# The recurrence branch's output projection: from block products inside the gate pairs to a stage of its own with seven products

## Chip, cores and metric

One core of one Trainium2 chip runs the whole kernel. The metric is device time in microseconds (us), the median of the runs.

## What is computed

One residual block in float32, for 1024 tokens of 1024 channels. Both branches read the same normalised input; what matters here is the merge:

```python
xn = rmsnorm(x, norm1_g)
u = xn @ w_in                      # q, k, v, f, i, q_hg, g_hg, gate_sb, gate_hg
o_sb = merge_heads(stick_breaking_attention(q_sb, k_sb, v_sb))        # 1024 x 512
o_hg = merge_heads(rmsnorm(hgrn2(...), hg_norm_g)) * silu(g_hg)       # 1024 x 512
g_a, g_b = sigmoid(gate_sb + b_a), sigmoid(gate_hg + b_b)
merged = g_a * (o_sb @ w_o_sb) + g_b * (o_hg @ w_o_hg)
h = x + merged @ w_out
h = h + square(relu(rmsnorm(h, norm2_g) @ w_ff1)) @ w_ff2
out = rmsnorm(h, final_g)
```

The change touches `o_hg @ w_o_hg`, a 1024 x 512 by 512 x 1024 product.

## The kernel before

Everything is kept with channels on partitions and tokens along the row. A float32 product is made of three matmuls of 128 x 128 weights on 512 tokens (`three`, L570): each operand is split into a rounded high part and the rest, and high x high, high x low and low x high are summed in a PSUM bank. The splits are `hi_lo` (L165): a cast on ScalarE (ACT, L157), then a subtraction on VectorE (DVE, L162). `load` (L136) issues loads on SyncE (SP), one behind the other; an instruction whose buffer or data isn't there yet holds back those behind it on its engine. Within an engine the order is that of the tile layer: it follows the code, with added edges by `after`, and buffers come from fixed pools, two each for the raw weights (`raw`), their high and low parts (`whi`, `wlo`), eight PSUM banks, 10 half tiles and 40 slots.

The large projections take seven products of half-size blocks in place of eight, with sums of weight blocks and of input blocks (forms). The gates' weight sums are made in DRAM by accumulating DMAs that GpSimd (POOL) issues, paced through the attention (`gate_weight_sums`, L1334; the sums `tw` for the output stage follow there, `out_weight_sums`).

**Gate pairs** (`GatePair`, from L1598). A pair cb makes 128 columns of both gates. Pairs 8 and 9 (named `gX8`, `gX9`) hold the gate g_hg of the recurrence and finish its four heads `on` (`ohg`); pairs 0 to 7 hold g_a and g_b and merge. The order is 8, 9, 0, 4, 1, 5, 2, 6, 3, 7 (L1773). Each runs, in the order of `gates` (L1783):

- `x6`: product 6 into bank gX; DVE makes gu = pr + gX, pr being partial products loaded from DRAM (12 matmuls).
- `y5`: product 5 into bank gY. Then `next_pair` splits the next pair's weights (wg, raw tiles of 1024 columns; whi/wlo and tgh/tgl their parts) and loads the one after.
- `x7`: product 7 onto gX; DVE reads gY (pr <- gY - pr, `pr<-gY,pr` in the profile), then gX twice; ACT takes sigmoids.
- `late_half`: for pairs 0 to 7 a block of 12 matmuls `pyh` (`hg_product`, L1655): 128 columns of `o_hg @ w_o_hg` for half of the tokens, 4 heads x 3. Its weights `wor` are loaded and split per pair (woh, wol), its inputs `a_hg` are the split heads (ahgh, ahgl). DVE multiplies and adds into y, which came with the attention branch's part (yr).
- `y3`: product 3 onto gY, so gY must have been read; DVE takes gu <- gY - gu, ACT the sigmoid.
- `early_half`: the other `pyh` block, and the merged result y; `out` (L1735) splits it (msh, msl) and, for pairs 4 to 7, makes forms (fs, yr) for the output stage.

So a pair of 0 to 7 has six blocks of 12 matmuls, four of gates and two of pyh. Behind pair 7 stands the output stage: banks pwW0 to pwW3 with a first product each, then a second each, and DVE adds and subtracts them to the residual rows h0 to h7 in between. Its weights are loaded into the raw buffers as wout11r, wout21r, wout2r and so on.

Of the kernel before, what the change touches and what calls it, by code (L numbers as in the profile page):

```python
# [20 lines left out]
P = 128  # L21
# [3 lines left out]
KT = D // P  # L25
# [15 lines left out]
def kernel(  # L41
# [1240 lines left out]

    a_sb, a_hg = Split("asb"), Split("ahg")
    mgs = Acts("ms")
# [49 lines left out]
    def gate_weight_sums():  # L1334
# [45 lines left out]
        yield from both(gh_sum(1, (0, 0), (0, 1)), (next(outs) for _ in range(2)))  # L1380
        yield from both(gh_sum(3, (0, 1), (1, 1)), (next(outs) for _ in range(2)))
        yield from outs

    def gate_sum(t, cb):
# [209 lines left out]
    class GatePair:  # L1594
# [3 lines left out]
        def load(self):  # L1598
# [7 lines left out]
            load(r1[:, 4:8], W_IN[512:, gate_cols(1, cb)].rearrange("(k p) c -> p k c", p=P))  # L1606
            if cb >= KT:
                return
            self.wo = half(f"wor{cb}")
            load(  # L1610
                self.wo.rearrange("p (k c) -> p k c", k=4),
                W_OHG[:, cb * P : (cb + 1) * P].rearrange("(k p) c -> p k c", p=P),
            )

        def load_sums(self):
            cb = self.cb
            self.p = slot(f"pr{cb}")
            load(self.p.rearrange("p (k t) -> p k t", k=2), pd[cb])
            if cb >= KT:
                load_g1(cb)  # L1620
                return
            self.y = slot(f"yr{cb}")
            load(self.y.rearrange("p (k t) -> p k t", k=2), yd[cb])

        def split(self, behind=None):
# [4 lines left out]
                slot(f"{t}g{cb}", F32R)  # L1630
                if self is gates_in[0]
                else wpool.tile([P, 1024], F32R, tag=t, name=f"{t}g{cb}")
# [6 lines left out]
            self.w.update({5: (h[:, s0], l[:, s0]), 7: (h[:, s1], l[:, s1])})  # L1639
            if cb >= KT:  # L1640
                return
            h, l = (half(f"wo{n}{cb}", F32R) for n in "hl")
            hi_lo(h, l, self.wo)
            self.hg = h, l

        def product(self, i, ps, start):
            open_block("fill")
            wh, wl = self.w[i]
            for k in range(4):
# [3 lines left out]
                three(ps, wh[:, ws], wl[:, ws], xh, xl, start and k == 0, k == 3, True)  # L1653

        def hg_product(self, i):  # L1655
            open_block("fill")
            ps = bank(f"pyh{self.cb}_{i}")
            for _ in proj_half(ps, self.hg, a_hg.mov, 4, i):
                pass
            return ps  # L1660

# [8 lines left out]
        def gated(self, which, first, second):  # L1670
            h = 2 * (self.cb - KT) + which

            def rest(u2_sum):
                if which == 1:
                    muls(u2_sum)
                a_hg.put(h, ohg[h], u2_sum)

# [99 lines left out]
    def next_pair(n, m, behind):  # L1777
        n.split(behind)
        n.load_sums()
        if m:  # L1780
            m.load()

    def gates():  # L1783
# [805 lines left out]
```

## Time and profile before

| | |
|---|---|
| median of 3 runs | 1421.53 us (1421.43 to 1423.29) |
| profiled execution | 1422.69 us, span 1420.9 us |
| clock granted to TensorE | 0.999 |
| PE (TensorE) busy | 1408.7 us, 99% |
| DVE busy | 1053.7 us, 74% |
| ACT busy | 683.6 us, 48% |
| pyh, first to last matmul | 596.9 to 719.1 us |
| output stage starts | 719.48 us |

Times in the trace count from the span's start. A row of the timeline gives start, duration, engine, line, operation and the tiles (written<-read); the chain of work that ended last gives start, length and group; a row of a window gives its length, then busy time and instructions of PE, PEld, DVE, ACT and POOL, the clock, and the DMA engines' busy share.

### The profile page before, as it was taken

Reading aid. Unit: us, or ns where it says so; the run is one execution under the profiler, and the core shown is the slowest. Engines: PE = TensorE matmul, PEld = TensorE weight load, DVE = VectorE, ACT = ScalarE, POOL = GpSimd, SP = SyncE. Lnnn points to the kernel's source line nnn. Section 1 sums busy time; section 2 is a strip of 40 time slices with the busy share of each in tenths; the row PEclk is TensorE's granted clock in tenths of the full one; section 3 lists DMA queues with packets and bytes.
Section 4 is the critical chain, followed back from the end, with each engine's and each line's share of the span. In section 5 each row is a group of like instructions: output and inputs, shape, how many; then the busy total and the mean of one; then the engine's idle time right before and its main releaser. Section 6 shows DMA issues by size and latency. Waiting matters only on the chain.

```text
span 1420.9 us, 18818 instructions
## 1 busy us (share of the span) xinstructions
PE 1408.7 (99%) x6848; PEld 1183.8 (83%) x6848; DVE 1053.7 (74%) x1443; ACT 683.6 (48%) x1183; POOL 191.1 (13%) x384
## 2 busy tenths in 40 slices
PE   9999999999999999999999999999999999999997
PEld 8888888888888888888888888888888888888886
DVE  7578898978556877866788897676666667768765
ACT  6366676664243544433244764445444443433343
POOL 3023222212232231000000300000000000000042
PEclk9999999999999999999999999999999999999999
DMA  7145766548767996465585514444446964776824
GB/s 241 42 82 114 153 167 133 121 131 182 182 144 177 296 240 225 140 216 170 163 303 193 185 57 166 163 163 146 138 143 244 355 256 159 270 283 235 282 93 174
DMA packets 175636, 260.26 MB, mean 183 GB/s; under 512 B 27020, under 2 KB 101304, under 8 KB 175544
## 3 DMA queue, kind: packets, MB, share of 16 engines
q1 hardware_dynamic: 146056, 190.37, 39.8%
q0 software_dynamic: 24048, 57.16, 17.9%
q10 hardware_dynamic: 5440, 11.54, 2.3%
q8 instruction: 54, 0.88, 0.2%
q14 instruction: 38, 0.31, 0.1%
HBM read 190.86 MB, written 88.60 MB: 197 GB/s over the span
## 4 chain that ended last, share of the span: by engine, by line
PE 97%; DVE 1%; ACT 1%; DMA 0%; POOL 0%; issue 0%; SPq 0%; POOLq 0%; DVEq 0%; ACTq 0%
PE pm L129 21%; PE pX L129 9%; PE pW L129 6%; PE pY L129 6%; PE pjqk L129 6%; PE gX L129 4%; PE gY L129 4%; PE pga L129 4%; PE pjf L129 3%; PE pjq L129 3%; PE pys L129 3%; PE pji L129 3%; PE pyh L129 3%; PE pjv L129 3%; PE po L129 3%; PE z L129 2%
## 5 line engine op out<-in xcount | busy, mean ns | idle before, releaser
L157 ACT CAST whid<-w 128x1024 fp32r<-128x1024 f32 x30 | 31.6, 1054 | 154.7 <-PE pm L129 90.1
L831 DVE TENSOR_TENSOR_SCAN rm<-rm,bits 128x511 f32<-128x511 f32 (+7 forms) x72 | 87.4, 1220 | 17.6 <-ACT rm L809 17.4
L129 PE MATMUL pm<-wlod,sh 128*128 128x512 f32 x240 | 93.5, 389 | 0.0
L129 PE MATMUL pm<-whid,sh 128*128 128x512 f32 x240 | 93.4, 389 | 0.0
L129 PE MATMUL pm<-whid,sl 128*128 128x512 f32 x240 | 93.4, 389 | 0.0
L129 PE MATMUL pm<-tl,sh 128*128 128x512 f32 (+1 forms) x210 | 81.3, 387 | 0.0
L129 PE MATMUL pm<-th,sl 128*128 128x512 f32 (+1 forms) x210 | 81.3, 387 | 0.0
L129 PE MATMUL pm<-th,sh 128*128 128x512 f32 (+1 forms) x210 | 81.3, 387 | 0.0
L2205 POOL TENSOR_SCALAR fss<-fss 128x1 f32<-128x1 f32 x8 | 4.5, 562 | 562.0 <-ACT fsc L2200 561.5
L162 DVE TENSOR_TENSOR wlod<-w,whid 128x1024 fp32r<-128x1024 f32 x30 | 36.7, 1222 | 54.0 <-ACT whid L157 54.0
L162 DVE TENSOR_TENSOR sl<-sa,sh 128x1024 fp32r<-128x1024 f32 x56 | 68.3, 1219 | 0.0
L157 ACT CAST wTh<-pw 128x128 fp32r<-128x128 f32 (+3 forms) x96 | 44.0, 486 | 42.7 <-PE pw L132 39.0
L157 ACT CAST sh<-sa 128x1024 fp32r<-128x1024 f32 x56 | 57.2, 1046 | 6.7 <-DMA sa<-ad 6.7
L162 DVE TENSOR_TENSOR wTl<-pw,wTh 128x512 fp32r<-128x512 f32 (+2 forms) x96 | 50.0, 546 | 7.1 <-ACT wTh L157 4.7
L129 PEld LDWEIGHTS pm<-wlod,sh 128*128 128x128 f32 x240 | 45.0, 187 | 9.8 <-DVE wlod L162 0.4
L129 PEld LDWEIGHTS pm<-whid,sl 128*128 128x128 f32 x240 | 45.1, 188 | 9.4
L129 PEld LDWEIGHTS pm<-whid,sh 128*128 128x128 f32 x240 | 45.0, 188 | 9.4
L170 DVE TENSOR_TENSOR bt<-bt,rm 128x511 f32<-128x511 f32 (+7 forms) x72 | 49.1, 685 | 4.0
L809 ACT ACTIVATE rm<-z 128x511 f32<-128x511 f32 (+4 forms) x96 | 48.2, 502 | 3.9 <-PE z L129 2.8
L129 PE MATMUL pX<-sqh,t1l 128*128 128x512 f32 x128 | 49.9, 390 | 0.0
L129 PE MATMUL pX<-sql,t1h 128*128 128x512 f32 x128 | 49.9, 390 | 0.0
L129 PE MATMUL pX<-sqh,t1h 128*128 128x512 f32 x128 | 49.8, 389 | 0.0
(894 smaller groups left out, 4447.8 us busy)
## 6 DMA issues: line engine op xcount, KB each, us to landing
w<-in_w_ff_dram SPq DMA_DIRECT2D x72, 512.0 KB, 4.7
sa<-ad SPq DMA_DIRECT2D x52, 512.0 KB, 6.2
tg<-in_w_in_dram POOLq DMA_DIRECT2D x35, 512.0 KB, 6.6
ad<-a SPq DMA_DIRECT2D x32, 256.0 KB, 4.5
ad<-s SPq DMA_DIRECT2D x16, 512.0 KB, 3.3
tw<-in_w_out_dram POOLq DMA_DIRECT2D x24, 256.0 KB, 7.2
pr<-pd SPq DMA_DIRECT2D x10, 512.0 KB, 6.7
x<-in_x_dram SPq DMA_DIRECT2D x8, 512.0 KB, 7.9
```

Source lines behind the costliest of these rows:

```text
L129: return pe(nc.tensor.matmul(*a, **k))
L157: hi_last[0] = after(in_turn("act", nc.scalar.copy(dst, src)), hi_behind[0])
L162: nc.vector.tensor_tensor(out=dst, in0=src, in1=hi.bitcast(F32), op=ALU.subtract),
L170: return nc.vector.tensor_tensor(out=out, in0=a, in1=b, op=ALU.mult)
L809: nc.scalar.activation(rm[:, s0 + c0 - 1 : s0 + m - 1], z[:, c0:m], AF.Sigmoid, scale=-0.125)
L831: sc = nc.vector.tensor_tensor_scan(out=rr, data0=rr, data1=bits[:, 1024 - nk + a : 1024 - nk + b][:, ::-1], initial=rm[:, b : b + 1] if i ...
L2205: nc.gpsimd.tensor_scalar(out=ssq, in0=ssq, scalar1=1.0 / D, scalar2=EPS, op0=ALU.mult, op1=ALU.add)
```

## The change

The pyh blocks, `wor` and `a_hg` go. In their place:

- `hg_weight_sums`: eight more accumulating DMAs of 512 KB each, which build sums of blocks of w_o_hg in DRAM (tv1 to tv4), one ahead of each of eight `tw` sums.
- `hg_forms`: the seven input forms, made out of the four heads in place on DVE (six subtractions, two additions) and split on ACT and DVE (hgh1 to hgh7, hgl1 to hgl7). Four of its steps are written behind gX0's `x6`, six behind `y5`, the rest behind product 3 of gY0.
- `hg_phase`, a stage behind the products of pair 0: four `HgPair`s (128 columns c and c + 512 each), every one with seven products of 2 x 3 matmuls into banks pyX, pyW and pyY; ACT copies bank contents (hp, hu, ht, hz), DVE combines them, and POOL and ACT store the four results per pair to DRAM (zd). Its weights are loaded as vb (6 x 128 columns) and va (8 x 128). The last products of HgPair 3 stand behind gX4's product 6.
- each gate pair loads its z (`zr`, 512 KB, on SP behind yr; pair 0's behind the first results, in `hg_phase`) and multiplies by it where it multiplied by pyh. Pair 4's weight parts are kept in slots.

A gate pair 1 to 7 so has four blocks of 12 matmuls, back to back: gX, gY, gX, gY. In the cut diff the class HgPair is left out but for its loads: per product it calls `three` for k = 0, 1, copies a bank on ACT (`kept`) and combines on DVE.

```diff
-    a_sb, a_hg = Split("asb"), Split("ahg")
+    a_sb = Split("asb")
...
+        yield from both(hg_weight_sums(), (next(outs) for _ in range(8)))
...
+    def hg_weight_sums():
+        def block(i, j):
+            return W_OHG[i * 256 : (i + 1) * 256, j * 512 : (j + 1) * 512]
+
+        for t, op, src in (
+            (1, ALU.bypass, block(0, 0)),
+            (3, ALU.bypass, block(0, 1)),
+            (1, ALU.add, block(0, 1)),
+            (3, ALU.add, block(1, 1)),
+            (2, ALU.bypass, tv[1]),
+            (2, ALU.add, block(1, 1)),
+            (4, ALU.bypass, tv[2]),
+            (4, ALU.add, block(1, 0)),
+        ):
+            paced(nc.gpsimd.dma_start(tv[t], src, accum_op=op))
+            yield
...
-            if cb >= KT:
-                return
-            self.wo = half(f"wor{cb}")
-            load(
-                self.wo.rearrange("p (k c) -> p k c", k=4),
-                W_OHG[:, cb * P : (cb + 1) * P].rearrange("(k p) c -> p k c", p=P),
-            )
...
-            self.y = slot(f"yr{cb}")
-            load(self.y.rearrange("p (k t) -> p k t", k=2), yd[cb])
+            if cb:
+                self.load_z()
+
+        def load_z(self):
+            self.y = slot(f"yr{self.cb}")
+            load(self.y.rearrange("p (k t) -> p k t", k=2), yd[self.cb])
+            self.z = slot(f"zr{self.cb}")
+            load(self.z.rearrange("p (k t) -> p k t", k=2), zd[self.cb])
...
-                if self is gates_in[0]
+                if self in (gates_in[0], gates_in[3])
...
-            h, l = (half(f"wo{n}{cb}", F32R) for n in "hl")
-            hi_lo(h, l, self.wo)
-            self.hg = h, l
...
-        def hg_product(self, i):
-            open_block("fill")
-            ps = bank(f"pyh{self.cb}_{i}")
-            for _ in proj_half(ps, self.hg, a_hg.mov, 4, i):
-                pass
-            return ps
...
-                a_hg.put(h, ohg[h], u2_sum)
+                    if h == 1:
+                        for _ in hg_split(1, (0, 1), 0):
+                            pass
...
-            ps = self.hg_product(1)
...
-            mul(p1, p1, ps)
+            mul(p1, p1, self.z[:, 512:1024])
...
-        def y3(self):
+        def y3(self, between=None):
             self.product(3, self.Y, False)
+            if between:
+                between()
...
-            ps = self.hg_product(0)
             y = self.y[:, 0:512]
-            mul(self.u2, self.u2, ps)
+            mul(self.u2, self.u2, self.z[:, 0:512])
...
+    def hg_split(m, heads, i):
+        if m not in hgf:
+            hgf[m] = tuple(slot(f"hg{n}{m}", F32R) for n in "hl")
+        for kk, h in enumerate(heads):
+            cs = slice(kk * 512, (kk + 1) * 512)
+            hi, lo = (t[:, cs] for t in hgf[m])
+            hi_lo(hi, lo, ohg[h][:, i * 512 : (i + 1) * 512])
+            yield
+
+    def hg_forms():
+        l, r = (cs for _, cs in halves())
+        yield from hg_split(2, (2, 3), 0)
+        yield from hg_split(4, (2, 3), 1)
+        for a, b in ((ohg[0], ohg[2]), (ohg[1], ohg[3])):
+            sub(b[:, r], a[:, r], b[:, r])
+            yield
+        for a in (ohg[0], ohg[1]):
+            sub(a[:, r], a[:, l], a[:, r])
+            yield
+        for a, b in ((ohg[0], ohg[2]), (ohg[1], ohg[3])):
+            sub(a[:, l], b[:, r], a[:, l])
+            yield
+        yield from hg_split(6, (0, 1), 0)
+        yield from hg_split(5, (2, 3), 1)
+        yield from hg_split(7, (0, 1), 1)
+        for a, b in ((ohg[0], ohg[2]), (ohg[1], ohg[3])):
+            add(b[:, l], b[:, l], a[:, l])
+            yield
+        yield from hg_split(3, (2, 3), 0)
...
+                (b[:, 0:4], W_OHG[:, c1]),
+                (b[:, 4:6], W_OHG[256:512, c2]),
+                (a[:, 0:4], tv13[:, c1]),
+                (a[:, 4:6], tv[2][:, c1]),
+                (a[:, 6:8], tv[4][:, c1]),
...
+    def hg_phase(v, n, m):
+        a, b, c, d = hgp
+        a.x1_w2()
+        a.x6_y5()
+        b.split_a()
+        c.load()
+        a.x7()
+        b.x1_w2()
+        c.split_b()
+        a.x4_y3()
+        v.load_z()
+        b.x6_y5()
+        c.split_a()
+        d.load()
+        b.x7()
+        c.x1_w2()
+        d.split_b()
+        b.x4_y3()
+        c.x6_y5()
+        d.split_a()
+        n.load()
+        c.x7()
+        d.x1_w2()
+        n.split()
+        n.load_sums()
+        m.load()
+        c.x4_y3()
+        d.x6_y5()
+        d.x7()
+        v.late_half()
+        v.early_half()
...
+            if v.cb == 0:
+                fs = hg_forms()
+                for _ in range(4):
+                    next(fs)
+                v.y5()
+                for _ in range(6):
+                    next(fs)
+                v.x7()
+                v.y3(lambda: [None for _ in fs])
+                hg_phase(v, n, m)
+                continue
+            if v.cb == 4:
+                hgp[3].x4_y3()
             v.y5()
-            if n and v.cb:
+            if v.cb == KT + 1:
+                next_pair(n, None, None)
+                hgp[0].load()
+                hgp[1].load()
+                hgp[0].split_b()
+                hgp[0].split_a()
+                hgp[1].split_b()
+            elif n:
                 next_pair(n, m, v.u2_sum if v.cb < KT else None)
-            elif not n:
+            else:
                 out_form["11"].split(1)
                 last_lo[0] = v.u2_sum
                 out_form["11"].split()
...
-            if not v.cb:
-                next_pair(n, m, v.y_sum)
```

Three places on DVE show what moves. The first is pair 0. Before, behind gX0's first reader (gu0), DVE finishes head on3 in two products, splits a head for `a_hg`, and reads gY0:

```order
L1289 TENSOR_TENSOR gu0_6024<-pr0_5961,gX0_6011 128x512
L170 TENSOR_TENSOR on3_5520<-on3_5520,gu9_5924 128x512
L170 TENSOR_TENSOR on3_5520<-on3_5520,pr9_5797 128x512
L162 TENSOR_TENSOR ahgl2_6027<-on2_5027,ahgh2_6026 128x1024
L1292 TENSOR_TENSOR pr0_5961<-gY0_6036,pr0_5961 128x512
```

After, from the same two products on3 on (gu0 stands one row ahead of them):

```order
L170 TENSOR_TENSOR on3_5538<-on3_5538,gu9_5941 128x512
L170 TENSOR_TENSOR on3_5538<-on3_5538,pr9_5816 128x512
L162 TENSOR_TENSOR hgl4_6066<-on2_5038,hgh4_6065 128x512
L162 TENSOR_TENSOR hgl2_6060<-on3_5538,hgh2_6059 128x512
L162 TENSOR_TENSOR hgl4_6066<-on3_5538,hgh4_6065 128x512
L1292 TENSOR_TENSOR on2_5038<-on0_4120,on2_5038 128x512
L1292 TENSOR_TENSOR on3_5538<-on1_4527,on3_5538 128x512
L1292 TENSOR_TENSOR on0_4120<-on0_4120 128x512
L1292 TENSOR_TENSOR on1_4527<-on1_4527 128x512
L1292 TENSOR_TENSOR on0_4120<-on2_5038,on0_4120 128x512
L1292 TENSOR_TENSOR on1_4527<-on3_5538,on1_4527 128x512
L1292 TENSOR_TENSOR pr0_5972<-gY0_6071,pr0_5972 128x512
```

Nine form operations (three splits, six subtractions in place) have come between on3 and the read of gY0, and the split of ahgl2 has gone.

The second is pair 2, behind pair 5. Before, from the first reader of gX2 to the read of gY2; wlog6, tgl6 and wol6 are low parts of pair 6's weights:

```order
L1289 TENSOR_TENSOR gu2_6515<-pr2_6420,gX2_6502 128x512
L162 TENSOR_TENSOR msl02_6260<-yr5_6307,msh02_6259 128x512
L162 TENSOR_TENSOR wlog6_6534<-wg6r1_6425,whig6_6533 128x1024
L1289 TENSOR_TENSOR yr5_6307<-yr5_6307,yr1_6180 128x512
L162 TENSOR_TENSOR tgl6_6538<-wg6r0_6424,tgh6_6537 128x1024
L162 TENSOR_TENSOR wol6_6542<-wor6_6429,woh6_6541 128x512
L1292 TENSOR_TENSOR pr2_6420<-gY2_6520,pr2_6420 128x512
```

After, the last twelve rows up to the same read; the two rows ahead of them are the first reader of gY5's last product (gu5) and yr5 times pr5:

```order
L1289 TENSOR_TENSOR yr5_6593<-yr5_6593,pr5_6591 128x512
L170 TENSOR_TENSOR gu5_6652<-gu5_6652,zr5_6595 128x512
L1292 TENSOR_TENSOR fs15_6707<-yr1_6496,yr5_6593 128x512
L1289 TENSOR_TENSOR yr5_6593<-yr5_6593,gu5_6652 128x512
L1292 TENSOR_TENSOR yr1_6496<-yr1_6496 128x512
L1289 TENSOR_TENSOR gu2_6745<-pr2_6676,gX2_6732 128x512
L1292 TENSOR_TENSOR yr1_6496<-fs15_6707,yr1_6496 128x512
L162 TENSOR_TENSOR msl02_6550<-yr5_6593,msh02_6549 128x512
L162 TENSOR_TENSOR wlog6_6764<-wg6r1_6683,whig6_6763 128x1024
L1289 TENSOR_TENSOR yr5_6593<-yr5_6593,yr1_6496 128x512
L162 TENSOR_TENSOR tgl6_6768<-wg6r0_6682,tgh6_6767 128x1024
L1292 TENSOR_TENSOR pr2_6676<-gY2_6750,pr2_6676 128x512
```

The split wol6 is gone; the end of pair 5's merge (yr5, fs15, yr1) stands closer, and its order around gu2 has changed. Pair 3 behind pair 6 reads the same but for one product less behind gu6; in pairs 1, 5, 6 and 7 at most one split of 1024 columns stands ahead of the read of gY.

The third is the change to the output stage. Before, the two splits of wout21r lie ahead of the reader of gY7's last product:

```order
L1289 TENSOR_TENSOR pr7_6789<-pr7_6789,gX7_6856 128x512
L162 TENSOR_TENSOR wout21l0_6983<-wout21r0_6978,wout21h0_6982 128x1024
L170 TENSOR_TENSOR pr7_6789<-pr7_6789,pyh7_1_6914 128x512
L170 TENSOR_TENSOR yr7_6791<-yr7_6791,pr7_6789 128x512
L162 TENSOR_TENSOR wout21l1_6987<-wout21r1_6980,wout21h1_6986 128x1024
L1289 TENSOR_TENSOR yr7_6791<-yr7_6791,pr7_6789 128x512
L1292 TENSOR_TENSOR gu7_6869<-gY7_6872,gu7_6869 128x512
```

After, that reader comes first:

```order
L1292 TENSOR_TENSOR gu7_7011<-gY7_7014,gu7_7011 128x512
L1289 TENSOR_TENSOR yr7_6957<-yr7_6957,pr7_6955 128x512
L162 TENSOR_TENSOR wout21l0_7099<-wout21r0_7094,wout21h0_7098 128x1024
L1292 TENSOR_TENSOR fs17_7059<-yr3_6860,yr7_6957 128x512
L170 TENSOR_TENSOR gu7_7011<-gu7_7011,zr7_6959 128x512
L1292 TENSOR_TENSOR yr3_6860<-yr3_6860 128x512
L1289 TENSOR_TENSOR yr7_6957<-yr7_6957,gu7_7011 128x512
L1292 TENSOR_TENSOR yr3_6860<-fs17_7059,yr3_6860 128x512
L162 TENSOR_TENSOR wout21l1_7103<-wout21r1_7096,wout21h1_7102 128x1024
L162 TENSOR_TENSOR msl03_6914<-yr7_6957,msh03_6913 128x512
L1292 TENSOR_TENSOR h4_7089<-h4_7089,pwW0_7109 128x512
L1289 TENSOR_TENSOR yr7_6957<-yr7_6957,yr3_6860 128x512
```

Both splits have moved behind the reader of gY7, the second by seven more operations. Behind these rows, in both kernels, stand the updates of h0, the two splits wout2l (whose loads use the buffers of the wout21 splits, in order), then the subtractions from h5 and h1 and the addition to h1 of bank pwW1.

On ACT the weight casts of the new stage stand among its copies: vbh3, hz1 and its store, whiv3, hu2 in this order, and later whig4, tgh4, hz2 and its store, hu3. On SP the order is that of `hg_phase`: yr0, zr0, vb3, va3, wg4r, pr4.

More of the change, by code (lines that the diff above doesn't have):

```diff
@@ L1381, in gate_weight_sums @@
         yield from both(gh_sum(3, (0, 1), (1, 1)), (next(outs) for _ in range(2)))
+        yield from both(hg_weight_sums(), (next(outs) for _ in range(8)))
         yield from outs
+    tv13 = dram("tv13", [512, 512])
+    tv = {1: tv13[0:256], 3: tv13[256:512]}
+    tv.update({i: dram(f"tv{i}", [256, 512]) for i in (2, 4)})
+    zd = [dram(f"zd{cb}", [P, 2, 512]) for cb in range(KT)]
+    def hg_weight_sums():
[13 more added lines that the diff above has]
+            yield
     def gate_sum(t, cb):
@@ L1639, in split @@
             self.w.update({5: (h[:, s0], l[:, s0]), 7: (h[:, s1], l[:, s1])})
-            if cb >= KT:
-                return
-            h, l = (half(f"wo{n}{cb}", F32R) for n in "hl")
-            hi_lo(h, l, self.wo)
-            self.hg = h, l
         def product(self, i, ps, start):
@@ L1781, in next_pair @@
             m.load()
+    hgf = {}
+    def hg_split(m, heads, i):
[26 more added lines that the diff above has]
+        yield from hg_split(3, (2, 3), 0)
@@ new lines @@
+    hgp = [HgPair(cp) for cp in range(4)]
+    def hg_phase(v, n, m):
[29 more added lines that the diff above has]
+        v.early_half()
@@ L1785, in gates @@
             v.x6()
-            v.y5()
-            if n and v.cb:
+            if v.cb == 0:
[11 more added lines that the diff above has]
+                hgp[3].x4_y3()
+            v.y5()
+            if v.cb == KT + 1:
[6 more added lines that the diff above has]
+            elif n:
                 next_pair(n, m, v.u2_sum if v.cb < KT else None)
-            elif not n:
+            else:
                 out_form["11"].split(1)
```

62 lines of the change are left out of this document (added).

## The prediction

> **What bounds the kernel now.** I read the chain of work that ended last first, whole and then for 560 to 720 us, which holds the first gate blocks up to the output stage.
>
> ```profile
> span 1420.9 us, 18818 instructions
> ...
> PE 97%; DVE 1%; ACT 1%; DMA 0%; POOL 0%; issue 0%; SPq 0%; POOLq 0%; DVEq 0%; ACTq 0%
> ```
>
> ```profile
> 567.16 2.72 PE gX L129 x12
> ...
> 586.20 2.72 PE gY L129 x12
> 588.92 2.72 PE gX L129 x12
> 591.64 2.72 PE gY L129 x12
> 594.36 2.72 PE gX L129 x12
> 597.08 2.72 PE pyh L129 x12
> 599.80 2.72 PE gY L129 x12
> ...
> 719.48 5.67 PE pwW L129 x25
> ```
>
> The second fence is that chain: start, length, group. Each block of 12 matmuls starts where the one before ends, so no other engine is waited for: 2.72 us per 12, or .2267 us per matmul. Two things must be seen. A matmul that goes is worth its full time; and an engine that answers late will show as a gap of PE, since here there is none.
>
> **What goes and what comes on PE.** The tile view of pyh counts what the change removes.
>
> ```profile
> L129 PE MATMUL pyh<-ahgh,woh x64: 389/389/389, 596.9 to 718.6; 128*128 128x512 f32 x64
> ...
> L129 PE MATMUL pyh<-ahgl,woh x64: 389/389/389, 597.1 to 718.9; 128*128 128x512 f32 x64
> ...
> L129 PE MATMUL pyh<-ahgh,wol x64: 389/389/389, 597.4 to 719.1; 128*128 128x512 f32 x64
> ```
>
> Three times 64, or 192 matmuls, 16 blocks: 16 x 2.72 = 43.52 us. The new stage has 4 column pairs x 7 products x 2 k x 3 = 168 of the same shape: 168 x .2267 = 38.08 us. **PE alone: -5.44 us.** A product of the new stage takes 6 x .2267 = 1.36 us.
>
> **What the new order makes PE wait for.** With the blocks packed closer, every answer of DVE and ACT is due earlier. I go through the places where PE reuses a bank or a form, taking each engine's order from the code and its durations from these rows (start, duration).
>
> ```profile
> 588.96 0.69 DVE L1292 TENSOR_TENSOR gu<-gY,gu 128x512 f32<-128x512 f32 x1 [0.46 <-PE gY L129]
> ...
> 592.56 0.69 DVE L170 TENSOR_TENSOR on<-on,gu 128x512 f32<-128x512 f32 x1
> 593.17 0.69 DVE L170 TENSOR_TENSOR on<-on,pr 128x512 f32<-128x512 f32 x1
> 594.51 1.23 DVE L162 TENSOR_TENSOR ahgl<-on,ahgh 128x1024 fp32r<-128x1024 f32 x1 [0.65 <-ACT ahgh L157]
> 595.65 0.69 DVE L1292 TENSOR_TENSOR pr<-gY,pr 128x512 f32<-128x512 f32 x1
> ```
>
> ```profile
> 579.34 0.60 ACT L157 CAST woh<-wor 128x512 fp32r<-128x512 f32 x1
> ...
> 591.25 1.06 ACT L157 CAST whig<-wg4r 128x1024 fp32r<-128x1024 f32 x1 [0.94 <-DMA wg4r<-in_w_in_dram]
> ```
>
> On DVE a 512-column operation is followed .60 later by the next and ends after .69; a 1024-column one 1.14 (594.51 to 595.65) and 1.22. On ACT a cast is .60 and 1.06; two 512 casts in a row end some .5 apart.
>
> *First gate block, the forms.* gY0's third product (form 3) may not start before DVE has read gY0 (pr0<-gY0). Before, that read ends at 596.34, and a pyh block still lies between: gY0 goes on at 599.80, 3.46 later. In the changed order both covers are gone. PE wants the bank at 597.08, right behind gX0; and ahead of pr0<-gY0 stand the nine form operations shown. Up to on3's second product DVE keeps its times (gu9, on2, one 1024-column split, gu9 by its sigmoid: 588.96 + .60 + .60 + 1.14 + .60 = 591.9, as before; so 593.17, ending 593.86). Then the two casts of on3 on ACT, .60 and .5: hgl2 at 594.5, hgl4 at 595.1; six differences at .60: 595.7 to 598.7; pr0<-gY0 at 599.3, ending 600.0. **Stall 2.9 us**, DVE work alone. If DVE could take pr0<-gY0 first, it would be 0, and the form-6 casts would be late instead.
>
> *Gate blocks 2 and 3.* A gate block was 16.3 us on PE with its pyh blocks; now it is 4 x 2.72 = 10.88, while DVE loses only the split of wor (.60).
>
> ```profile
> 620.00:719.50 99.50, 99.50 (x440) 82.39 (x439) 69.63 (x98) 31.63 (x43) 7.56 (x14) 1.00 0.56 183
> ```
>
> The third pair of columns is DVE: 69.63 us busy in 99.5, which is six blocks and a little. Less five wor splits that is 66.5 us of work, for six blocks of 10.88 = 65.3. So DVE has as much to do as PE, and its order decides. From the end of gY5's last product to the end of pr2<-gY2 stand 14 operations, two of 1024 columns: 11 x .60 + 2 x 1.14 + .69 = 9.6 us, while PE has gX2, gY2, gX2 to do, 8.16 us, before it wants gY2 back: 1.4. Two operations of which one needs the other's result lie .73 apart (718.40 to 719.13, below), which adds some .3: 1.7. From gY6's last product to pr3<-gY3 there are 13, hence 1.1. In pairs 1, 5, 6 and 7 at most one split of 1024 columns stands ahead of the read, and the sum stays under 8.16. **Stall 2.8 us.**
>
> *Out stage.* pwW1's second product may start when DVE has updated h1 with pwW1's first one. Five blocks behind gY7's end, P, it is due: P + 13.6. Ahead of that update DVE's order has the splits of wout2r, whose second load waits for the split of wout21 in the same buffer.
>
> ```profile
> 715.35 1.22 DVE L162 TENSOR_TENSOR wout21l<-wout21r,wout21h 128x1024 fp32r<-128x1024 f32 x1
> ...
> 717.09 0.68 DVE L1292 TENSOR_TENSOR gu<-gY,gu 128x512 f32<-128x512 f32 x1
> ...
> 718.40 0.69 DVE L1292 TENSOR_TENSOR yr<-yr 128x512 f32<-128x512 f32 x1
> 719.13 0.69 DVE L1292 TENSOR_TENSOR yr<-fs,yr 128x512 f32<-128x512 f32 x1
> ...
> 724.84 2.35 DVE L162 TENSOR_TENSOR wout2l<-wout2r,wout2h 128x1024 fp32r<-128x1024 f32 x2
> ...
> 728.30 0.68 DVE L1289 TENSOR_TENSOR h<-h,pwW 128x512 f32<-128x512 f32 x1
> ```
>
> ```profile
> 713.80 3.17 SPq L137 DMA_DIRECT2D wout2r<-tw  x2
> ```
>
> ```profile
> pr<-pd SPq DMA_DIRECT2D x9, 512.0 KB, 6.7
> yr<-yd SPq DMA_DIRECT2D x8, 512.0 KB, 6.6
> ...
> wor<-in_w_o_hg_dram SPq DMA_DIRECT2D x8, 256.0 KB, 5.1
> yd<-ys ACTq DMA_DIRECT2D x5, 256.0 KB, 4.1
> ...
> wout11r<-in_w_out_dram SPq DMA_DIRECT2D x2, 512.0 KB, 8.1
> ...
> wout2r<-tw SPq DMA_DIRECT2D x2, 512.0 KB, 6.6
> ...
> wg2r<-tg SPq DMA_DIRECT2D x1, 512.0 KB, 4.0
> ...
> wg4r<-in_w_in_dram SPq DMA_DIRECT2D x1, 256.0 KB, 3.4
> ```
>
> (The last is the list of DMA issues in 540 to 740: size, and us to landing.) Before, both wout21 splits stand ahead of gu7<-gY7, the second load of wout2r is issued as the second ends (713.80 + 3.17 less the issue itself), and h1 is done at 728.98, 4.1 ahead of 733.08. Now the second split stands eight operations behind P: .60 + .60 + 1.14 + 5 x .60 + 1.22 = P + 6.6. Load 6.6, cast 1.06, split 1.14, three updates 1.9: P + 17.3. **Stall 3.7 us.** With 4.0 for the load it is 1.1, with 8.1 it is 5.2.
>
> *The round trip of z.* The results go out to zd and come back as zr. The load of zr0 stands on SP ahead of vb3, va3 and wg4r, and waits until hz0's store has landed. From E, the end of the product that hz0 copies: copy .6, store 4.1, zr0's issue and two of vb3 1.0, vb3's landing 5.1 (wor is the same weights), then on ACT vbh3 .8, hz1 .5, whiv3 1.0, hu2 .6, and up to .7 for whiv2 ahead of hz0: E + 13.7 to 14.4. X2's product 7 waits for hu2 and is due ten products behind E, 13.6: .1 to .8. Then zr0 lands (6.6) and DVE, which stands at pr0<-zr0, does seven operations and the split wlov3 (5.7), which frees the buffer for wg4r's second load (.5 + 3.4); ACT casts both halves of it ahead of hu3: X3's product 7 is some 1.4 late. **I take 2.3 us**; with the shortest loads shown 0, with 1 us more for each of the four transfers 4.8.
>
> *vb1.* pr0 can be issued at gX8's end, 569.88; vb1's second part is issued when pr0 has landed (6.7) and lands at 581 to 581.7; vbh1, hgh2 and the sigmoid of gu8 follow on ACT (2.0), two operations on DVE (1.3), then gX9 goes on: 584.3 to 585 against 583.48, and .6 more at gY9. **I take 1.5 us**; 0 with loads of 4, 3.4 with 8.
>
> *Hidden.* The 8 sums of 512 KB on POOL move the last tw sums by eight places, in a stretch in which the DMA engines have no room:
>
> ```profile
> 480.00:520.00 40.00, 40.00 (x218) 34.38 (x217) 31.21 (x51) 17.89 (x39) 15.23 (x20) 1.00 1.03 270
> ```
>
> Their DMA share is 1.03, but PE does not idle, and the sums are read 60 us later: I take 0, from a gain of nothing to one block's loss of 2.7 if a transposed input comes late. The new copies on ACT lie under a busy share of a third.
>
> **Sum.** -5.44 + 1.5 + 2.9 + 2.8 + 2.3 + 3.7 = **+7.8 us**. Against the profiled execution (1422.69, 1.8 of it outside the span) that is 1430.5; the median of the runs shown stands 1.2 below it, so **1429.3**. Behind the out stage PE is the chain again, so nothing is given back.
>
> **Rivals.**
> *Fast loads.* If loads land like the fastest rows (4.0 and 3.4), vb1 and the round trip cost 0 and the out stage 1.1: -5.44 + 2.9 + 2.8 + 1.1 = +1.4, or 1422.9 on the median. Against it: the medians of nine, eight and two transfers are 6.7, 6.6 and 6.6, and zd, zr and the new weight loads add 9.6 MB net in the same stretch (4 + 4 + 3.6, less 2 of wor). The Trainium skill, "DMA: Bandwidth & Descriptors", section "Anatomy of one DMA — SWDGE (gpsimd) path", fits a transfer as about 2 us plus its bytes at 436 GB/s, an estimate of 3.2 us for 512 KB; by that rule the sum would be about +0.6; this trace's 6.7 for 512 KB disagrees. Chance .14.
> *The full gain: faster.* One mechanism: DVE's pr<-gY comes in time in blocks 0, 2 and 3, and loads are short. It decides at 597.08: if DVE has read gY0 by then and has no lag later, PE keeps its 24 matmuls: 1416.1. For it: DVE is busy 70% before the change. Against: six differences and two casts cannot fit between 593.86 and 597.08 (4.9 us of work). Chance .09; with only the forms' stall (-2.5, 1419.0) another .03.
> *Heavier traffic.* All the upper ends: -5.44 + 3.4 + 2.9 + 2.8 + 4.8 + 5.2 = +13.7, or 1435.2, and with the 2.7 of the sums 1438. Chance .08.
>
> **Chances.** Forecast .66 (1424.4 to 1434). About 0.2%, 2.8 us, is what a measurement of this kernel can tell from no change: faster .09, same .17 (fast loads and the forms alone), slower .74. The range 1420 to 1437 leaves out the full gain and the last of the heavy traffic, some .14.
>
> **What would show it.** Groups pyX, pyY and pyW of 168 matmuls in all in place of pyh; idle of PE ahead of gY0 released by DVE pr (2.9), of gY2 and gY3 by DVE pr (1.7, 1.1), of pwW by DVE h (3.7), of pyX by ACT hu (2.3), of gX9 and gY9 by DVE (1.5). The forecast is wrong if PE shows no idle at gY0, or if vb3, zr0 and wout2r land within 4 us.

## The result, and the profile after

The changed kernel takes **1436.3 us** (median of 4 runs, 1434.37 to 1439.62) against 1421.95 for the kernel before beside it: a ratio of 1.0102, 95% interval 1.0081 to 1.0122. So it is about 14 us slower, where 7.8 was forecast. The first lines of its page, span and chain:

```profile
span 1434.9 us, 18939 instructions
...
PE 86%; DMA 4%; DVE 4%; issue 2%; ACT 2%; POOL 1%; SPq 0%; POOLq 0%; ACTq 0%; DVEq 0%
```

PE held 97% of the chain before and holds 86% now; transfers, DVE and ACT have 10% of it. This is the path followed back from the end, not idle time: PE is busy for 1409.0 us, as long as before (1408.7) with 24 matmuls fewer. The place is found with five marks that both traces have (start of the matmul; the last column is the end of the last one):

| stage | before | after | difference |
|---|---|---|---|
| start to the last po (attention) | 327.8 | 326.8 | -1.0 |
| last po to the first gX | 228.2 | 234.9 | **+6.7** |
| first gX to the first pwW | 163.3 | 167.7 | **+4.4** |
| first pwW to the first pwX | 21.8 | 27.4 | **+5.6** |
| first pwX to the last matmul | 672.0 | 671.7 | -0.3 |

(Behind the last matmul 7.8 us follow before and 6.5 after, so the spans differ by 14.0.) Three stages lose time, and the first of them ends before any product of the new stage runs. What PE waited for in 340 to 760 us (us in all, times, longest); before, this view is empty over the same stretch:

```profile
PE gY L129 <- DVE pr L1292: 5.7, 4, 2.8
PE pwW L129 <- DVE h L1289: 3.7, 1, 3.7
PE pot L132 <- DVE hon L170: 3.3, 2, 2.5
PE sl L129 <- DVE q L170: 1.7, 1, 1.7
PE sl L129 <- ACT ksl L1067: 1.2, 1, 1.2
PE gX L129 <- DVE gu L1289: 0.4, 1, 0.4
```

The first two rows are the waits that were forecast; pot and sl lie in the recurrence, at 415 to 561 us, and were not. The pauses seen one by one, in the chain (start, length, group):

```profile
602.61 3.61 DVE on L1292 x6
606.23 0.61 DVE pr L1292
606.88 4.60 PE gY L129 x12
...
691.88 0.61 DVE pr L1292
692.54 3.01 PE gY L129 x12
...
714.96 0.61 DVE pr L1292
715.62 3.02 PE gY L129 x12
...
736.15 6.44 DMA wout2r<-tw
742.67 1.06 ACT wout2h L157
...
746.16 0.61 DVE h L1289
746.82 10.07 PE pwW L129 x36
```

Read them in pairs: six form operations and then pr0 ahead of gY0; pr2 and pr3 ahead of gY2 and gY3; wout2's load, its cast and h ahead of pwW. Two lengths are new: 12 matmuls behind the pause at gY0 take 4.60 us instead of 2.72, and 36 in pwW 10.07 instead of 8.16. The matmuls themselves, in the timeline behind gY0's pause:

```profile
606.88 0.50 PE L129 MATMUL gY<-gsh,whig 128*128 128x512 f32 x1 [2.78 <-DVE pr L1292]
...
608.22 0.63 PE L129 MATMUL gY<-gsl,whig 128*128 128x512 f32 x1
608.64 0.63 PE L129 MATMUL gY<-gsh,wlog 128*128 128x512 f32 x1
...
611.33 0.40 PE L129 MATMUL pyX<-hgh,vbh 128*128 128x512 f32 x1
611.56 0.39 PE L129 MATMUL pyX<-hgl,vbh 128*128 128x512 f32 x1
```

The slow ones follow each other by .43 instead of .23 (starts), and the granted clock of the windows (the third value from the end) says why:

```profile
606.90:608.90 2.00, 2.00 (x6) 1.63 (x7) 2.00 (x4) 1.86 (x4) 0.00 (x0) 0.66 0.05 12
608.90:611.00 2.10, 2.10 (x6) 1.64 (x6) 2.10 (x5) 1.53 (x3) 0.00 (x0) 0.51 0.00 0
```

The clock is halved for some seven matmuls: a pause of 2.78 us has cost 2.78 + 1.88, of which about .3 is the restart that every pause costs (last section).

The pause at 415 us, on POOL:

```profile
407.69 0.99 POOL L1404 DMA_DIRECT2D tv<-in_w_o_hg_dram  x1
...
415.25 0.52 POOL L1404 DMA_DIRECT2D tv<-tv  x1 [4.56 <-DMA tv<-in_w_o_hg_dram]
415.84 0.19 POOL L266 TENSOR_SCALAR hss<-hss 128x4 f32<-128x4 f32 x1
416.11 1.04 POOL L270 TENSOR_TENSOR hn_y<-hss,expo 128x4 f32<-128x4 f32 x1
```

The copy of tv1 into tv2 stands in POOL's queue until the sum issued at 407.69 has landed, at 414.97. Behind it stand hss and hn_y, the norm of a recurrence head, which DVE (hon) and then PE (pot) wait for.

The pauses at 527 and 533 us (sl) have another way. DVE stands at gs, which reads the transposed input xnl, and the operands q and k of sl come behind it on DVE:

```profile
523.90 1.23 DVE L1292 TENSOR_TENSOR gs<-xnl,xnl 128x1024 f32<-128x1024 f32 x1 [7.28 <-DMA xnl<-xnh]
```

Before, the same wait is 2.04. The slowest of the six transfers of xnl in this stretch takes 21.2 us from issue to landing, against 16.1 before and 14.6 in e9, and POOL now issues eight more tw sums between 506 and 542 us, next to these transfers. So of the 6.7 us 2.5 are a wait in POOL's queue and 2.8 (1.18 + 1.65) late transposed inputs; a pause of .79 at 561 and the restarts make the rest. That it is the tw sums that make xnl late is not shown by itself.

### The profile page after: what moved, and what is told of

The parts are those of the page before. It is cut to its first block, busy times and chain, and to the rows that moved or that the text cites. A ratio compares the mean times of both kernels' runs of the same rounds, so it can differ in the third digit from the quotient of the medians.

```text
span 1434.9 us, 18939 instructions
## 1 busy us (share of the span) xinstructions
PE 1409.0 (98%) x6824; PEld 1180.8 (82%) x6824; DVE 1071.6 (75%) x1474; ACT 699.5 (49%) x1210; POOL 198.0 (14%) x404
## 4 chain that ended last, share of the span: by engine, by line
PE 86%; DMA 4%; DVE 4%; issue 2%; ACT 2%; POOL 1%; SPq 0%; POOLq 0%; ACTq 0%; DVEq 0%
PE pm L129 21%; PE pX L129 9%; PE pW L129 6%; PE pY L129 6%; PE pjqk L129 5%; PE pga L129 3%; PE pji L129 3%; PE pjq L129 3%; PE pjv L129 3%; PE po L129 3%; PE pjf L129 3%; PE gY L129 3%; PE gX L129 2%; PE pwX L129 2%; PE z L129 2%; PE pw L132 2%
```

## The experiments

**Theory:** the 14 us are three things: pauses of PE where DVE's order puts other work ahead of the read that frees a bank; the half clock behind some of these pauses; and the eight weight sums, which hold up POOL's queue. **Rivals:** the bytes count and not the place of the sums; DVE is full, so that a pause taken away comes back later. Medians of the runs are given, but several edits are smaller than the spread of the changed kernel (1434 to 1440), so the stages decide. They are read from one profiled execution of each kernel. Last po to gX, gX to pwW, pwW to pwX, pwX to the last matmul:

| kernel | median us | ratio to before (95%) | po-gX | gX-pwW | pwW-pwX | behind |
|---|---|---|---|---|---|---|
| before | 1421.95 | | 228.2 | 163.3 | 21.8 | 672.0 |
| changed | 1436.3 | 1.0102 (1.0081 to 1.0122) | 234.9 | 167.7 | 27.4 | 671.7 |
| e1 sums left out | 1429.8 | 1.0050 (1.0035 to 1.0065) | 228.1 | 167.3 | 27.7 | 672.0 |
| e2 sums last | 1442.16 | 1.0141 (1.0124 to 1.0158) | 239.6 | 167.7 | 27.0 | 672.0 |
| e3 forms behind | 1436.57 | 1.0094 (1.0079 to 1.0109) | 236.8 | 163.7 | 25.7 | 672.0 |
| e4 pause filled | 1438.16 | 1.0113 (1.0096 to 1.0130) | 235.3 | 167.6 | 24.9 | 672.0 |
| e5 tg split behind | 1438.35 | 1.0107 (1.0093 to 1.0121) | 234.5 | 164.3 | 29.3 | 672.0 |
| e6 wout2 behind | 1436.9 | 1.0103 (1.0087 to 1.0118) | 237.4 | 165.8 | 21.8 | 675.2 |
| e9 sums early | 1430.71 | 1.0051 (1.0038 to 1.0065) | 228.0 | 167.3 | 25.0 | 672.0 |
| e10 = e9+e3+e5+e6 | 1425.72 | 1.0019 (1.0010 to 1.0028) | 228.0 | 161.2 | 21.8 | 677.9 |
| e11 wout2 in slots | 1433.49 | 1.0079 (1.0065 to 1.0093) | 236.3 | 165.6 | 23.7 | 672.0 |
| e12 = e9+e3+e5+e11 | 1424.97 | 1.0016 (1.0007 to 1.0025) | 228.2 | 160.4 | 24.8 | 672.0 |
| e13 = e12, whole split behind | 1423.09 | 1.0004 (0.9995 to 1.0013) | 228.0 | 161.6 | 23.4 | 672.0 |
| e14 = e13, wout2 split later | 1421.22 | 0.9987 (0.9978 to 0.9996) | 227.9 | 164.5 | 21.8 | 671.7 |

**e1, the sums left out.**

```diff
-        yield from both(hg_weight_sums(), (next(outs) for _ in range(8)))
...
-                (a[:, 0:4], tv13[:, c1]),
+                (a[:, 0:4], W_OHG[:, c2]),
...
```

> Leaves out the eight sums of w_o_hg's blocks (va is loaded from plain blocks of w_o_hg, so the new stage works with other weights); everything else is as in the changed kernel. Theory: PE's four gaps before the gate pairs (2.52 at 415, 1.18 and 1.65 around 530, 0.79 at 561: 6.1 us, none of them in before) come from these sums, which stand in POOL's queue ahead of the normalisation steps and of the transposed inputs' transfers. All four go: about 6 us less, some 1430. Rival: the gaps are what the execution happened to have, or come from the other transfers that were moved: they stay, and the time stays at 1436. The gaps at gY0, gY2, gY3 and pwW (2.8, 1.6, 1.0, 3.7) stay in both.

The stage up to gX is back at 228.1, and PE does not pause in it: the list of its waits from 340 to 560 us is empty (window: length, then PE's busy time; first the changed kernel, then e1):

```profile
440.00:560.00 120.00, 117.17 (x634) 99.87 (x633) 83.43 (x131) 58.35 (x130) 39.75 (x55) 1.00 0.94 244
```

```profile
440.00:560.00 120.00, 120.00 (x643) 102.21 (x642) 89.98 (x138) 63.70 (x137) 35.01 (x46) 1.00 0.92 243
```

The 6.7 us are the sums' own; the pauses at gY0 and in pwW stay.

**e2, the sums behind all others.**

```diff
-        yield from both(hg_weight_sums(), (next(outs) for _ in range(8)))
         yield from outs
+        yield from hg_weight_sums()
```

> The same eight sums, but behind all the sums of w_out instead of one ahead of each of eight. Theory (place in POOL's queue): the gap at 415, where a copy of tv1 into tv2 waits at the head of POOL's queue until the sum of tv1 has landed and a normalisation step waits behind it, goes (-2.5); around 530 the late transfers are now the sums of w_o_hg themselves, so those gaps may stay: 1431 to 1434. Rival (bytes): only the amount moved counts, the gaps add up to about 6 us as before, wherever they lie: 1436.

Both numbers missed: the pause at 415 is gone as the theory says, but the whole is slower, 1442.16. What PE waited for in 340 to 570, and POOL ahead of it:

```profile
PE pot L132 <- DVE hon L170: 9.2, 2, 8.7
```

```profile
551.09 0.51 POOL L1404 DMA_DIRECT2D tv<-tv  x1 [7.72 <-DMA tv<-in_w_o_hg_dram]
...
556.70 0.93 POOL L1404 DMA_DIRECT2D tv<-in_w_o_hg_dram  x1 [4.54 <-DMA tv<-tv]
...
558.27 0.19 POOL L266 TENSOR_SCALAR hss<-hss 128x4 f32<-128x4 f32 x1
```

With nothing between them, each sum waits at the head of POOL's queue for the one before to land (7.72, 4.54), and the norm of the last head stands behind the chain. The bytes are the same and the loss is 11.4 us instead of 6.7: it is the place and the chain that count.

**e9, the sums in the attention.** They are issued one every fourth step, where the DMA engines' share is .55 in the changed kernel and .61 now.

```diff
-        yield from both(hg_weight_sums(), (next(outs) for _ in range(8)))
...
+    hsums = hg_weight_sums()
...
         if i % 2 == 0:
             next(wsums, None)
+        if i % 4 == 1:
+            next(hsums, None)
```

> The eight sums of w_o_hg are issued one every fourth step of the attention, far ahead of the stretch in which the DMA engines are full; everything else is as in the changed kernel. Theory (place in POOL's queue, between the recurrence's normalisation steps): from the end of attention to the first gate pair the time falls from 234.9 to 228 us, the whole to about 1429.6, as with the sums left out, since the DMA engines have room there (share 0.55 up to 300 us). Rival (bytes): the sums delay the other sums, and the gaps come in the attention or again around 530: less than half of the 6.7 is won.

228.0 us up to gX, as with none, and 1430.71: met, and the rival by bytes falls. It takes both losses away at once, the wait in POOL's queue and the late inputs; no run parts the two.

**e3, forms behind product 7.**

```diff
                 v.y5()
+                v.x7()
                 for _ in range(6):
                     next(fs)
-                v.x7()
                 v.y3(lambda: [None for _ in fs])
```

> The six subtractions of the input forms are written behind product 7 of pair 0, so that DVE reads gY0 four operations after on3 instead of ten. Theory (DVE's order, and a clock that drops after such a pause): the gap ahead of gY0's product 3 (2.78) shrinks to under 0.5, and the twelve matmuls behind it take 2.7 us instead of 4.60: 4 to 4.7 us less, about 1432. Rival 1: the gap goes but the slow matmuls have another cause: 2.8 less. Rival 2: form 6 is now late and the same gap stands ahead of pyX0's product 6: no gain.

The pause at gY0 is gone and its block is 2.72; the stage from gX to pwW falls by 4.0, of which some .5 comes back at pyX0's product 7, where hu's copy stands on ACT behind six casts of the late forms (.21, the first of the two waits in the last row, and a restart):

```profile
603.95 2.72 PE gY L129 x12
```

```profile
PE gY L129 <- DVE pr L1292: 2.9, 3, 1.6
PE pwW L129 <- DVE h L1289: 2.0, 1, 2.0
PE pyX L129 <- ACT hu L1875: 0.5, 2, 0.3
```

The median does not show it (1436.57). The profiled execution lost as much more ahead of gX (3.6 in the attention, 1.9 behind it) as it won behind it, so the stage is the evidence here.

**e4, the pause filled** with 12 matmuls whose bank is not read.

```diff
                 v.x7()
+                spare = bank("spare")
+                v.product(7, spare, True)
                 v.y3(lambda: [None for _ in fs])
```

> Twelve matmuls more, a product 7 of pair 0 into a spare bank that nothing reads, between product 7 and product 3 of pair 0, where PE pauses for 2.78 us. Theory (the clock drops because PE pauses): the pause is filled, gY0's product 3 starts when it did, and its twelve matmuls take 2.72 instead of 4.60: 1.9 us less although 2.7 us of matmuls are added. Rival: they are slow for another reason (DVE's or ACT's reads, the bank): they stay at 4.60, and the time stays the same or grows by up to 2.7.

gY0's block takes 2.85 instead of 4.60 (starts of its first matmul and of the one behind its twelve):

```profile
608.14 0.50 PE L129 MATMUL gY<-gsh,whig 128*128 128x512 f32 x1
...
610.99 0.39 PE L129 MATMUL pyX<-hgh,vbh 128*128 128x512 f32 x1
```

But the stage is no shorter (pauses at gX9 and pyX were .4 and .9 longer here), nor is the median. And e5, e6 and e11 have the same pause of 2.78 or 2.79 at gY0 without a slow block; that alone makes their stage from gX to pwW 1.6 us shorter. So e4 agrees with the clock's account and does not settle it alone; the pauses of all the runs, in the last section, carry it.

**e5, the second split of the next weights behind the read of gY.**

```diff
-                next_pair(n, m, v.u2_sum if v.cb < KT else None)
+                if v.cb < KT:
+                    n.split(v.u2_sum, True)
...
             v.x7()
+            if n and v.cb < KT:
+                n.split_r0(v.y_sum)
+                n.load_sums()
+                if m:
+                    m.load()
```

> In gate pairs 0 to 7 the split of the first half of the next pair's weights (tgh, tgl) and the loads behind it are written behind product 7, so that one 1024-column split fewer stands on DVE ahead of the read of gY. Theory (DVE's order): 13 operations or 8.4 us stand against 8.16 of PE ahead of gY2, 12 or 7.8 ahead of gY3: the gaps there fall from 1.6 and 1.0 to 0.3 and 0, 2.3 to 3 us less between the first gate pair and the output stage. Rival (DVE is full over the whole stretch): the same operations come a little later and the gaps move to other pairs, as late products 6 or 5: no gain.

The pauses at gY2 and gY3 fall from 1.61 and 1.02 to .48 and .45, and the stage by 3.35 (1.6 of it because no slow block followed gY0's pause). But pwW's pause grew to 5.9 (wout2's second cast came 3.2 us after DVE was ready), and nothing is won in all:

```profile
PE pwW L129 <- DVE h L1289: 5.9, 1, 5.9
```

**e6, wout2 behind the updates of h.**

```diff
             if tb == 0:
-                out_operands(["2"])
                 load_rows(6, 2, 7, 3)
+            if tb == 3:
+                out_operands(["2"])
```

> The weights wout2 are loaded and split behind all four updates by pwW's first products instead of behind the first. Theory (the updates of h stand on DVE behind splits that wait for a load): the gap inside pwW (3.7, and 1.9 by the slow clock behind it) goes, and the stage from pwW to pwX falls from 27.4 to 22 us; 5.6 less. Rival: wout2 now comes late for pwX: the gap stands ahead of pwX instead, and the time stays.

pwW to pwX falls to 21.8, as forecast, and the rival is right too: 3.2 us come back behind it, since wout3's loads need the same two buffers.

```profile
PE pwX L129 <- DVE h L1292: 1.5, 1, 1.5
```

**e10, all of it.**

> All edits together: sums early, forms behind product 7 of pair 0, tg splits behind product 7 of the pairs, wout2 behind the updates. Theory: of the 14 us lost, 6.7 by the sums, 4.4 at gY0, 2.6 to 3 at gY2 and gY3 and 5.6 at pwW come back, and what stays is the change's own 24 matmuls less, -5.4, and 1 to 2 us of small gaps: 1417 to 1419, faster than both kernels. Rival (DVE full from the first pair to the output stage): the gaps come back elsewhere, and the time stays above 1422.

1425.72, above the forecast: 6 of the 14 us that were to come back moved behind pwX (677.9 instead of 672.0), as the rival says.

```profile
PE pwX L129 <- DVE h L1292: 1.7, 1, 1.7
PE hnt L132 <- DVE hn L2017: 1.7, 1, 1.7
```

**e11, wout2's raw weights in slots** (of which the forms' leave some free), so that their load no longer waits for wout21's split.

```diff
+            if n == "2":
+                out_form[n].roomy = (0, 1)
             out_form[n].split()
```

> The changed kernel, with wout2's raw weights loaded into two free slots instead of the two raw buffers that wout21 holds; the order of the code stays. Theory (the updates of h stand behind splits that wait for a load which waits for wout21's second split): the load comes early, DVE goes from that split through wout2's to the updates, P + 6.6 + 2.7 + 2.3 + 1.9 = P + 13.5 against 13.6: the gap in pwW goes from 3.7 to at most 0.5, pwW to pwX takes 22 us instead of 27.4, and the stages behind keep their 672 us, since nothing is moved behind: 5 us less. Rival 1 (the DVE work itself is late): a gap of 2 us or more stays. Rival 2: the time comes back behind pwX, as it did with the later split.

The pause in pwW is 1.65 instead of 3.71, pwW to pwX 23.7, and 672.0 behind it: nothing is pushed on. The median is 2.8 us lower where 5 were expected. Neither the theory's .5 nor the first rival's 2 us came, and the rest is not DVE's work, as that rival has it, but the load again:

```profile
729.66 10.62 DMA wout2r<-tw
```

```profile
740.14 2.52 DVE L162 TENSOR_TENSOR wout2l<-wout2r,wout2h 128x1024 fp32r<-128x1024 f32 x2 [1.27 <-ACT wout2h L157]
```

It is issued earlier and takes 10.62 us instead of 6.44, with the DMA engines' share at .99 in 729 to 741. DVE is idle for 1.27 of the 1.65 us, waiting for the cast of what it brings.

**e12 and e13.** e12 takes e9, e3, e5 and e11 together; e13 splits the other half of the next weights behind the read of gY too.

```diff
             self.y_sum = sub(p1, self.Y, p1)
+            if between:
+                between()
...
-                    n.split(v.u2_sum, True)
...
-            v.x7()
+            v.x7((lambda: n.split(v.y_sum, True)) if n and v.cb < KT else None)
```

> Sums early, forms behind product 7 of pair 0, tg splits behind product 7 of the pairs, and wout2 in slots at its old place in the code. Theory: 228 us up to the first gate pair, 161.2 from there to pwW, 22 to pwX, 672 behind: 2 us less than before in all, some 1419.5 to 1421. Rival: DVE's lag out of the gate pairs makes the updates late in pwW or pwX, as behind the later split (677.9 instead of 672): 1424 or more.

> As the kernel with sums early, forms behind, tg splits behind and wout2 in slots, but the other half of the next pair's weights (whi, wlo) is split behind DVE's read of gY too. Theory (order): the last gaps of 0.48 at gY2 and gY3 go, each with the 0.3 of a restart: 1.5 us less from the first pair to pwW, 159.7. Rival (DVE is as full as PE in the pairs): the next pair's product 6 waits for wlo instead, and the stretch stays at 161 or grows.

e12 missed at pwW (24.8 instead of 22), and its time is the rival's, 1424 or more. With e13 the pauses at gY2 and gY3 went, but two came at the next product 6 and behind it (.5 and .8), as its rival says, and the stage is no shorter:

```profile
PE pwW L129 <- DVE h L1289: 1.4, 1, 1.4
PE gX L129 <- DVE gu L1289: 0.8, 1, 0.8
PE gX L129 <- DVE wlog L162: 0.5, 1, 0.5
```

wout2's load takes 11.11 us in e13's chain (716.71 on), when the DMA engines are full (share 1.01 in 717 to 732), and 11.83 in e12's. Ahead of its splits DVE is idle for .97 us in e13 and 1.67 in e12, so of the pauses in pwW (1.37 and 2.70) an estimated 1.0 and 1.7 are the load and .4 and 1.0 DVE's own lag.

**e14, loaded there but split behind the updates.**

```diff
-                out_operands(["2"])
+                out_form["2"] = out_unit("2", tw[2])
+                out_form["2"].roomy = (0, 1)
+                out_form["2"].load()
                 load_rows(6, 2, 7, 3)
+            if tb == 3:
+                out_form["2"].split()
```

> As the kernel with sums early, forms behind, both halves of the next pair's weights split behind DVE's read of gY and wout2 in slots; wout2 is loaded at the same place as there, but split behind all four first updates of h, so that a late load no longer holds the updates. Theory (head of DVE's queue): the gap of 1.4 to 2.7 in pwW goes, pwW to pwX falls from 23.4 to 21.8, and the stages behind keep 672, since wout3's loads no longer wait for wout2's buffers: 1.5 us less than without it, about 1421.5, level with or just under before. Rival (DVE is behind on its whole work): the lag turns up at pwX or in the norm, as with the later load (677.9), and the time is 1423 or more.

Met: 21.8 in pwW, 671.7 behind it, and 1421.22 against 1422.92 beside it, 0.13% faster than before (interval 0.9978 to 0.9996) and 1% faster than the change as made. Its profiled execution shows where the 5.44 us went, small pauses of which each costs .3 more (last section):

```profile
PE gX L129 <- DVE gu L1289: 2.0, 2, 1.2
PE pyX L129 <- ACT hu L1883: 1.5, 3, 0.8
PE gX L129 <- DVE wlog L162: 0.5, 1, 0.5
PE gY L129 <- DVE pr L1292: 0.3, 1, 0.3
```

4.3 us of pauses and seven restarts of .3, 6.4 in all, is more than the 24 matmuls are worth; this execution took 1423.16 us, near the upper end of its kernel's eleven (1420.07 to 1423.6).

## Why the prediction was half right

The direction and the part of the mechanism that lies on DVE held, the size did not: +14.35 against +7.8. The time is above the forecast's 1424.4 to 1434 and .7 inside the range's end at 1437. That it is inside owes something to luck: two terms came 3 us cheaper than summed and hid as much of the loss. Term by term (pause, then what the restart and the slower matmuls behind it add):

| step | forecast | measured |
|---|---|---|
| 24 matmuls fewer | -5.44 | -5.44 (6848 to 6824 on PE) |
| vb1, gX9 and gY9 | 1.5 | .38 + .29, and .6 |
| gY0, forms | 2.9 | 2.78, and **1.88** |
| gY2 and gY3 | 2.8 | 1.61 + 1.02, and .6 |
| round trip of z | 2.3 | .12, and .3 |
| pwW | 3.7 | 3.71, and **1.91** |
| weight sums ("Hidden") | 0 | **6.7** |

Measured, these add up to +16.5; the three stages lost 16.7. The attention (-1.0), the stages behind pwX (-.3) and the time behind the last matmul (-1.3) bring the spans to about +14.

- *What bounds it, and the order of DVE.* Right. The three pauses that were summed from DVE's order and its pitch of .60 came within .2 us: 2.78 for 2.9, 2.63 for 2.8, 3.71 for 3.7. In pwW the parts came too: wout21's second split ended 6.8 behind gY7 for 6.6, and the load took 6.44 for 6.6. e3, e5 and e11 show that they hang on that order and, in pwW, on the load.
- *"Hidden. ... I take 0, from a gain of nothing to one block's loss of 2.7".* This is the step that failed: the 0 has no better reason than that the sums are read late and that PE did not idle before. They cost 6.7. Its own upper end, a transposed input that comes late, was paid (2.8). And it weighed the sums as DMA traffic alone. They are also instructions in POOL's queue, and one that waits holds up the head norm behind it, which PE soon needs (2.5). e1 removes the loss, e2 enlarges it with the same bytes, e9 removes it with the same bytes elsewhere.
- *The price of a pause.* The sum took a pause at its length. Behind gY0 and in pwW the clock fell to half, 1.9 us each with the restart, and each other pause costs some .3 for its restart. Together 5.3 us. At gY0 the slow clock hangs on where the pause lies (last section): e5, e6 and e11 have the pause and not the 1.6.
- *Round trip and vb1.* Sized too high: 0.8 of pauses instead of 3.8. Both hang on loads, and these vary: gX9's pause is below .1 in e12, .38 here and 1.18 in e14, and the two behind the round trip in e14 are .76 and .50. Here the load of zr0 was issued 2.2 us behind hz0's store (626.01 and 623.81), where the sum had 4.1 for the store.
- *The rivals.* Fast loads and the full gain did not come. The measured time lies where the heavier traffic was put (1435), but not by its terms: vb1, the round trip and pwW paused for .7, .1 and 3.7 instead of 3.4, 4.8 and 5.2. Only the late transposed input, which it adds for 1438, came true. The fit of the Trainium skill that *Fast loads* quotes is, by its section's title, for DMAs that GpSimd issues; the 6.7 us beside it are of loads on SP and do not test it.

What stays open: how much of the sums' 6.7 us goes with either way alone, since e1 and e9 remove both; and the 1.0 us in the attention and the 1.3 behind the last matmul, which nothing here explains.

## What to carry to other kernels

Where PE runs without a pause, the matmuls that an algebraic form saves are worth only what the other engines' orders leave: go through each read that frees a bank and count what stands ahead of it, and price a pause with what the clock adds. A DMA that waits is an instruction like any other: look at what stands behind it on the engine that issues it, and at the transfers that it pushes back, not only at its bytes. An edit judged alone may vanish in a pause further on; compare stages, not only totals.

## What the runs showed of the hardware

- **The clock halves behind a pause of PE, but not by its length alone.** In the changed kernel and its twelve variants, from 300 us on: none of the pauses up to 1.69 us was followed by slow matmuls; of 16 between 2.05 and 3.16 us 7 were and 9 were not; all six from 3.35 us were. The same pause of 2.78 at gY0 came with slow matmuls in the changed kernel and without in e6. What decides is how much of the pause falls into one step of a fixed grid. In each trace the stretches at half clock last 3.41 us (in e2 once three in a row) and start whole multiples of 3.413 us apart: 607.53 and 747.48 in the changed kernel are 41 steps apart (where a trace has none earlier, the one behind its last matmul gives the grid). With the time cut into these steps, the pause lies in one step there and is parted in e6 (window: length, PE's busy time, clock, DMA share; first the changed kernel, then e6):

```profile
604.12:607.53 3.41, 0.65 (x3) 1.00 0.43 123
607.53:610.95 3.42, 3.42 (x10) 0.50 0.03 7
```

```profile
604.50:607.91 3.41, 2.40 (x11) 1.00 0.82 231
607.91:611.33 3.42, 1.66 (x7) 1.00 0.16 45
```

From 300 us to the last matmul, in all thirteen traces, 15 steps have 2.05 us or more of idle PE, and a step at half clock follows each of them; it follows none of the others, which have up to 1.94. (One more, at 170 us in e3, followed a step with 1.75, so the bound is not sharper than that.) The Trainium skill, "TensorE: Matmul & The Clock Gate", section "Part 1: The HAM clock gate (the "warmup" mystery)", puts the halving after at least one idle window of about 3.4 us on a free-running count. The free-running count and its length agree with these traces; that 2.05 us of idle in a step was enough does not fit a whole idle window.
- **A pause costs some .3 us more than its length even at full clock:** the blocks of 12 behind pauses of 1.0 to 1.6 us took 3.02 and 3.01 instead of 2.72, the first matmul .50 instead of .39. About half of it is lost overlap: a matmul lasts .39 and the next one otherwise starts .23 behind its start.
- **The same load can take nearly twice as long:** wout2's 512 KB took 6.44 us in the changed kernel's chain (DMA share .92 in 735 to 747) and 10.62 to 11.83 in e11 to e13 (.99 to 1.01).
